# An encoder block's input stage: table times for the first eight tiles of x, two half tiles in other PSUM banks, copies of the first tokens moved

## The chip, the cores and the metric

The kernel runs on one core of a Trainium2 chip, as one program. The metric is the device time of one execution in microseconds (us), lower is better. Engines are named as in the profile: PE (TensorE; PEld its weight loads), DVE (VectorE), ACT (ScalarE), POOL (GpSimd), SP (SyncE, which issues all DMAs here).

## The reference

One encoder layer over x of 2048 tokens x 1024: a normalisation, one wide projection, two attention mixers, gates, three more projections. What the change touches is the first line, and the use of its result in the gate columns `ga`, `gb`:

```python
h = rms_norm(x, norm_gain)          # x * rsqrt(mean(x*x) + EPS) * gain
proj = h @ w_in
qa, ka, va, qb, kb, vb, ga, gb, mg = split(proj)
ya = banded_attention(...) * silu(ga)
yb = dilated_attention(...) * silu(gb)
gates = sigmoid(mg + b_merge)
y = x + (gates0 * (ya @ w_branch_a) + gates1 * (yb @ w_branch_b)) @ w_out
```

## The kernel before

**The input stage.** x is cut into 16 tiles of 128 tokens. Every matmul operand is split into a high and a low fp16 half, so that three fp16 products (high x high, low x high, high x low) stand for one fp32 product; the transposed x is kept in SBUF as `XH` and `XL` (1024 channels x tokens). A tile goes through these steps:

- `x_square` (L448, ACT): squares of the tile and their sum.
- `x_stats` (L452, L261, DVE; two small instructions) and `x_newton` (three Newton steps to the reciprocal root) for a group of tiles together. `rs_newton` makes nine small DVE instructions (L275 to L277) for the groups of two and twelve small POOL instructions (L270 to L273) for the groups of four. The groups are tiles 0-1, 2-3, 4-7, 8-11, 12-15.
- `x_scale` (L462, DVE): the tile (128x1024 fp32, SBUF to SBUF) times its factor.
- `x_turn` (L468, PE): four 128x128 transposes of a half tile (512 channels) into one of three PSUM banks "s". "(t,h)" below is half h of tile t; there are 32.
- `x_hi` (L471, ACT) copies the half tile from PSUM to fp16 `XH`; `x_lo` (L475, DVE) subtracts that from PSUM and writes `XL`.
- `x_again` (L479, POOL) copies the first two tiles' columns of `XH` and `XL` behind the last token (four copies).

**Beside it**, three column blocks of the gate weights (gate 0, 1, 2) are prepared: `g_gain` (L324, POOL, two halves), `g_square` (L332, ACT), `g_sum` (L194, PE), `g_pow` (L201 to L345, seven small DVE instructions), `g_hi` (L350, ACT), `g_lo` (L354, DVE); and the first unit's weights, with `w_gain` (L180, POOL, four quarters), `w_square` (L219, ACT) and others. `warm(n)` puts n matmuls of constants on PE (L502).

**The gates.** When the 512 tokens of quarter q (four tiles) are transposed, gates 0 and 1 of that quarter follow: 24 matmuls each (L308: `XH` by `gh`, `XL` by `gh`, `XH` by `gl` for eight channel blocks), then `tanh` (L371, ACT), `gate` (L378, DVE) and a store. Four quarters make 192 matmuls. Behind them begin the projections of the first unit (L651).

**What sets the order.** Every engine runs its own queue in order, and waits where an operand isn't ready. The program is recorded once on the host: `at(t, f)` puts step f on a heap under a planned time t, `until(t)` records all steps that are planned up to t, and `stream` records the 24 matmuls of a gate over 5.2 planned us with `until` between them. So the constants `X_...` are no waits: they only say in which order the instructions stand on each queue. In the version before, the planned time of a tile's scaling is a straight line in t, and everything of the tile hangs on it:

```python
def scale_time(t):
    return X_CH[0] + X_CH[1] * t
b = scale_time(t) + X_CH[2] + X_CH[5] * h
at(b, x_turn, t, h)
at(b + X_CH[3], x_hi, t, h)
at(b + X_CH[3] + X_CH[4], x_lo, t, h)
```

Of the kernel before, what the change touches and what calls it, by code (L numbers as in the profile page):

```python
# [32 lines left out]
NT = S // 128  # L33
# [47 lines left out]
Y_MAX = (0.026, 0.815, 0.839)  # L81
X_SQ = (5.098, 1.401, 9.779, 2.051)
X_CH = (9.3, 2.65, 1.024, 0.955, 1.155, 1.305)
X_ST = (1.3, 0.179)
X_G = (7.5, 15.282, 45.87)
X_GP = (2.1, 5.694, 7.094, 7.694, 8.894, 10.194)
X_W = (14.0, 38.0, 48.0, 1.1, 4.8, 5.2, 6.3, 0.6, 50.255)
X_WARM = (24, 16, 16, 16, 12)
X_TH = (0.8, 2.173, 3.5)
# [22 lines left out]
def block_kernel(tc, x, w_units, w_gate, w_mrg, w_brn, w_out, w_bra, gain, qkg, sink, bias_a, bias_b, b_merge, out):  # L112
# [326 lines left out]

    groups = {0: (0, 1), 1: (0, 1), 2: (2, 3), 3: (2, 3)}  # L440
    groups.update((t, tuple(range(t - t % 4, t - t % 4 + 4))) for t in range(4, NT))

# [21 lines left out]
    def x_turn(t, h):  # L464
        xps[t, h] = ps = s_p.tile([128, 4, 128], F32, name="s")
        for c in range(4):
            cc = 4 * h + c
            T.transpose(ps[:, c, :], xts[t][:, 128 * cc:128 * cc + 128], idf[:])  # L468

    def x_hi(t, h):  # L470
        A.activation(XH[:, 4 * h:4 * h + 4, 128 * t:128 * t + 128], xps[t, h][:], AF.Copy)  # L471

    def x_lo(t, h):
        ts = slice(128 * t, 128 * t + 128)
        V.tensor_tensor(XL[:, 4 * h:4 * h + 4, ts], xps[t, h][:], XH[:, 4 * h:4 * h + 4, ts], OP.subtract)  # L475
        done.add(("x", t, h))
# [35 lines left out]
    def scale_time(t):  # L512
        return X_CH[0] + X_CH[1] * t

    def ready_time(t):
        return scale_time(t) + sum(X_CH[2:])

    for t, n in enumerate(X_WARM):
        at(scale_time(t) + X_CH[2] - .05 if t < 4 else scale_time(3) + X_CH[2] + X_CH[5] + .05, warm, n)
    for t in range(NT):  # L520
        b = X_SQ[0] + X_SQ[1] * t if t < 4 else X_SQ[2] + X_SQ[3] * (t - 4)
        at(b, x_square, t)
        if t == groups[t][-1]:
            at(b + X_ST[0], x_stats, groups[t])
            at(b + X_ST[0] + X_ST[1], x_newton, groups[t])
        b = scale_time(t)
        at(b, x_scale, t)
        for h in range(2):
            b = scale_time(t) + X_CH[2] + X_CH[5] * h
            at(b, x_turn, t, h)  # L530
            at(b + X_CH[3], x_hi, t, h)
            at(b + X_CH[3] + X_CH[4], x_lo, t, h)
        if t < 2:
            for k in range(2):
                at(ready_time(t) + 1.0 + 1.2 * k, x_again, t, (XH, XL)[k])
        if t + XT_BUFS < NT:
            at(ready_time(t), x_load, t + XT_BUFS)
    for c in range(3):
        b = X_G[c]
        if c == 2:  # L540
            at(X_G[0] + X_GP[5] + .1, g_load, c)
        chain([(b + X_GP[0] * i, g_gain, c, i) for i in range(2)]
              + [(b + d, f, c) for d, f in zip(X_GP[1:], (g_square, g_sum, g_pow, g_hi, g_lo))])
    at(X_W[0], w_load, 0)
# [16 lines left out]
    for q in range(4):  # L561
# [1185 lines left out]
```

## Time and profile before

| | |
|---|---|
| time, median of 3 runs | 1960.59 us (1957.21 to 1961.2) |
| the profiled execution's own time | 1960.34 us |
| its span (first to last instruction) | 1958.6 us |
| busy: PE / DVE / ACT / POOL | 99% / 70% / 54% / 49% of the span |
| mean granted TensorE clock | 0.996 |
| first gate matmul, first matmul of the first unit | 28.60 us, 80.79 us after the span's start |

The profiled execution is 1.74 us longer than its span, and 0.25 us under the median. The busy shares are over the whole span; the change lies within its first 81 us, so what counts is what each engine waits for there.

### The profile page before, as it was taken

How to read it: one execution, taken by the hardware profiler on the slowest of the kernel's cores; microseconds unless marked ns; L12 is line 12 of the kernel's file. 1: busy time of each engine (PE TensorE's matmuls, PEld its weight loads, DVE VectorE, ACT ScalarE, POOL GpSimd, SP SyncE). 2: the span in 40 equal slices, each digit the busy share in tenths (PEclk: the TensorE clock that was granted, in tenths of full speed). 3: DMA queues.
4: the chain of work that ended last, by engine and by line, in shares of the span. 5: the costliest groups of instructions: out<-in, count | busy, mean ns of one | idle time of the engine just before them, and what ended most of it. 6: DMA issues, size and time to landing. Idle time of an engine off the chain costs nothing.

```text
span 1958.6 us, 48091 instructions
## 1 busy us (share of the span) xinstructions
PE 1935.7 (99%) x17606; PEld 1392.0 (71%) x17606; DVE 1377.4 (70%) x3604; ACT 1059.8 (54%) x2415; POOL 956.0 (49%) x2440
## 2 busy tenths in 40 slices
PE   8999999999999999999999999999999999999999
PEld 5567896677788898888989889899544444444444
DVE  6668777888768776667876878767776757876312
ACT  7457656776565566565666655656534545432100
POOL 4254556455546656647566676656511210232533
PEclk8999999999999999999999999999999999999999
DMA  6239987797848596677777776755822346788763
GB/s 250 81 81 168 194 150 159 141 187 141 177 101 184 118 185 126 125 148 164 152 132 154 135 169 126 143 118 118 187 81 85 106 165 195 218 241 268 252 228 145
DMA packets 589773, 308.46 MB, mean 157 GB/s; under 512 B 458080, under 2 KB 527328, under 8 KB 588256
## 3 DMA queue, kind: packets, MB, share of 16 engines
q1 hardware_dynamic: 589536, 305.39, 67.0%
q8 instruction: 137, 2.24, 0.5%
q14 instruction: 100, 0.82, 0.1%
HBM read 129.91 MB, written 65.27 MB: 100 GB/s over the span
## 4 chain that ended last, share of the span: by engine, by line
PE 80%; DVE 6%; POOL 6%; issue 4%; ACT 2%; DMA 2%; SPq 0%; POOLq 0%; DVEq 0%; ACTq 0%
PE pj L651 32%; PE pj L308 14%; PE fps L308 13%; PE fps L1614 7%; PE fps L1409 5%; PE s L805 4%; PE pv L854 4%; POOL rs_t L270 1%; DVE rw L715 1%; POOL rs_t L271 1%; DVE qss L703 1%; POOL rs_t L272 1%; POOL rw L722 1%; POOL rs_y L273 1%; PE pt L916 1%
## 5 line engine op out<-in xcount | busy, mean ns | idle before, releaser
L651 PE MATMUL pj<-wl,XH 128*128 128x128 f16 (+2 forms) x2816 | 715.2, 268 | 0.0
L651 PE MATMUL pj<-wh,XH 128*128 128x128 f16 (+2 forms) x2816 | 708.7, 268 | 4.0 <-DVE vt L691 4.0
L651 PE MATMUL pj<-wh,XL 128*128 128x128 f16 (+2 forms) x2816 | 711.6, 269 | 0.0
L651 PEld LDWEIGHTS <-XH 128*128 128x128 f16 x5632 | 574.6, 113 | 64.7 <-issue 5.8
L651 PEld LDWEIGHTS <-XL 128*128 128x128 f16 x2816 | 318.1, 113 | 26.7 <-issue 0.5
L820 DVE CUSTOM_DVE_ANT_0 pr<-s,b,ubuf 128x256 f32<-128x256 f32 (+3 forms) x512 | 218.6, 464 | 48.6 <-PE s L805 47.0
L270 POOL TENSOR_TENSOR rs_t<-rs_y 128x8 f32<-128x8 f32 (+2 forms) x345 | 105.4, 306 | 207.5 <-DVE rs_y L261 142.7
L837 DVE SCALAR_TENSOR_TENSOR p<-pr,p 128x512 f16<-128x512 f32 (+2 forms) x256 | 185.0, 723 | 21.6 <-ACT p L833 21.1
L308 PEld LDWEIGHTS <-wh 128*128 128x128 f16 x960 | 93.7, 98 | 111.0 <-issue 1.5
L715 DVE TENSOR_TENSOR rw<-rw,qr 128x512 f32<-128x512 f32 (+1 forms) x112 | 111.6, 997 | 86.7 <-POOL vt L678 58.4
L722 POOL TENSOR_TENSOR rw<-rw,g 128x128 f32<-128x128 f32 (+1 forms) x224 | 131.1, 605 | 78.1 <-DVE rw L715 62.1
L833 ACT ACTIVATE p<-pr 128x512 f16<-128x512 f32 (+2 forms) x256 | 159.5, 623 | 7.1 <-issue 0.3
L670 ACT ACTIVATE rw<-pj 128x256 f32<-128x256 f32 (+1 forms) x224 | 86.5, 386 | 134.3 <-PE pj L651 133.4
L737 POOL COPY spl<-spl 128x256 f16<-128x256 f16 (+1 forms) x224 | 93.7, 448 | 127.2 <-DVE spl L732 125.7
L308 PE MATMUL fps<-Y,wh 128*128 128x512 f16 x512 | 152.2, 379 | 0.0
L805 PE MATMUL s<-kq 128*128 128x128 f16 (+1 forms) x1856 | 147.3, 218 | 1.5 <-DMA kq<-spl 1.4
L805 PEld LDWEIGHTS <-kq 128*128 128x128 f16 x2016 | 129.8, 98 | 25.1 <-issue 2.0
L308 PE MATMUL pj<-XH,gh 128*128 128x512 f16 x384 | 145.5, 379 | 0.0
L308 PE MATMUL pj<-XH,gl 128*128 128x512 f16 x384 | 145.5, 379 | 0.0
L308 PE MATMUL pj<-XL,gh 128*128 128x512 f16 x384 | 145.5, 379 | 0.0
L1614 PE MATMUL fps<-wt,M 128*128 128x512 f16 (+1 forms) x684 | 145.2, 375 | 0.0
L728 ACT ACTIVATE spl<-rw 128x512 f16<-128x512 f32 (+1 forms) x112 | 72.1, 644 | 126.2 <-POOL vt L678 87.0
(241 smaller groups left out, 3702.2 us busy)
## 6 DMA issues: line engine op xcount, KB each, us to landing
wraw<-in_w_units_dram SPq DMA_DIRECT2D x56, 384.0 KB, 4.6
mtd<-mm SPq DMA_DIRECT2D x56, 256.0 KB, 3.7
M<-mtd SPq DMA_DIRECT2D x8, 1792.0 KB, 9.5
mgd<-fg SPq DMA_DIRECT2D x39, 256.0 KB, 2.1
zd<-z SPq DMA_DIRECT2D x128, 66.0 KB, 1.9
zz<-zd SPq DMA_DIRECT2D x64, 132.0 KB, 2.9
xt<-in_x_dram SPq DMA_DIRECT2D x16, 512.0 KB, 8.9
gtd<-yo SPq DMA_DIRECT2D x32, 256.0 KB, 2.7
```

The costliest lines, as they stand in the source:

```text
L270: G.tensor_tensor(tv, yv, yv, OP.mult)
L308: out.append(lambda w=w, xx=xx, ch=ch, i=i: T.matmul(ps[:], lhsT=w[:, ch, c0:c0 + 128], rhs=xx[:, ch, ts], start=(i == 0), stop=(i == n - 1)))
L651: out.append(lambda lhs=lhs, rhs=rhs, ch=ch, a=a, b=b, k=k: T.matmul(ps[:, a:b], lhsT=lhs[:, ch, :], rhs=rhs[:, ch, a:b], start=(k == 0), ...
L715: V.tensor_tensor(q, q, self.rr[:, :n].unsqueeze(2).to_broadcast([128, n, HD]), OP.mult)
L722: G.tensor_tensor(q[:, i, :un.nq, :], q[:, i, :un.nq, :], g, OP.mult)
L737: G.tensor_copy(sp[:, i, nh:, :, :], sp[:, i, nq:nh, ::-1, :])
L805: T.matmul(self.sv[j][:, o:o + k1 - k0], lhsT=q[:, h, :], rhs=kt[:, un.nq + kh + v * un.nk, k0:k1], start=(v == 0), stop=(v == 1))
L820: V.tensor_tensor_reduce(out=self.pv[:, j, self.p0:self.p0 + W], in0=self.sv[j], in1=un.bias[:, self.h0 + j, self.b0:self.b0 + W], scale=I ...
L833: A.activation(self.sp[:, :128 * n], self.pr, AF.Copy, scale=PSC)
L837: V.scalar_tensor_tensor(self.sp[:, 128 * n:], self.pr, PSC, self.sp[:, :128 * n], OP.mult, OP.subtract)
L1409: mm.append(lambda ch=ch, k=k, w=w, i=i: T.matmul(ps[:], lhsT=weight(bl, ch)[w], rhs=xblock(x, ch)[k], start=(i == 0), stop=(i == 11)))
L1614: mm.append(lambda ch=ch, k=k, w=w, i=i: T.matmul(ps[:, :cols.stop - cols.start], lhsT=m[:, a, ch, k, :], rhs=wt[w][:, b, ch, cols], start ...
```

## The change

The straight line is replaced by tables for the tiles 0 to 7: `X_SQ`, `X_SC`, `X_NW`, `X_TU`, `X_HI`, `X_LO` give each step a planned time of its own; tiles 8 to 15 follow a line again, with other constants. Tiles 4-5 and 6-7 become groups of two, whose Newton steps stay on POOL (`g[0] > 2`). The half tiles (1,1) and (2,0) are transposed into the two banks "pj", in which the gates accumulate later. The four `x_again` copies get planned times behind the quarter 1 gates. The 84 `warm` matmuls become 86, of which 60 stand ahead of the first transpose. A gate's matmuls are recorded no earlier than its weights' planned time. Nothing that is computed changes.

```diff
--- before.py
+++ after.py
@@ -79,13 +79,22 @@
 N_PREP = (6.3, 7.15, 7.753)
 B_GAP = (0.25, 0.138, 0.231)
 Y_MAX = (0.026, 0.815, 0.839)
-X_SQ = (5.098, 1.401, 9.779, 2.051)
-X_CH = (9.3, 2.65, 1.024, 0.955, 1.155, 1.305)
-X_ST = (1.3, 0.179)
-X_G = (7.5, 15.282, 45.87)
-X_GP = (2.1, 5.694, 7.094, 7.694, 8.894, 10.194)
-X_W = (14.0, 38.0, 48.0, 1.1, 4.8, 5.2, 6.3, 0.6, 50.255)
-X_WARM = (24, 16, 16, 16, 12)
+X_SQ = (4.7, 6.0, 7.67, 9.519, 13.423, 20.123, 22.646, 24.708, 27.708, 1.508)
+X_SC = (9.358, 10.138, 12.938, 13.688, 24.438, 25.089, 28.349, 29.268, 39.768, 2.218)
+X_NW = (7.25, 10.067, 20.868, 26.596, 36.596, 45.765)
+X_TU = (10.2, 10.9, 11.6, 12.3, 13.8, 14.493, 15.2, 15.9)
+X_HI = (11.3, 12.649, 13.349, 14.068, 16.645, 17.245, 17.49, 18.804)
+X_LO = (14.5, 15.675, 16.352, 17.052, 19.152, 20.901, 20.452, 20.869)
+X_WARM = (60, 0, 6, 12, 8)
+X_WT = (-1.003, 11.5, 13.892, 16.492, 19.692)
+X_AGAIN = 48.907
+X_CH = (1.024, 0.955, 1.155, 1.238)
+X_ST = 1.7
+X_G0 = (9.8, 13.049, 14.349, 16.349, 18.756, 20.691)
+X_G1 = (14.336, 20.174, 22.209, 22.874, 23.774, 25.779)
+X_G2 = (46.672, 54.444, 55.393, 56.249, 57.893, 59.393)
+X_GD = 1.863
+X_W = (17.0, 38.0, 50.417, 1.1, 4.956, 7.803, 8.828, 3.203, 53.849)
 X_TH = (0.8, 2.173, 3.5)
 T_Y = (2.0, 0.8, 1.6, 1.5, 4.0, 26.0, 0.5, 1.3, 2.1, 1.6, 2.0)
 T_P = ((0, 0.0, 0.03), (1, 3.0, 50.0), (2, 56.0, 75.0), (3, 82.0, 102.0), (4, 108.5, 128.3))
@@ -437,8 +446,8 @@
         V.tensor_scalar(bmh[:], bmt[:], 0.5, None, OP.mult)
 
 
-    groups = {0: (0, 1), 1: (0, 1), 2: (2, 3), 3: (2, 3)}
-    groups.update((t, tuple(range(t - t % 4, t - t % 4 + 4))) for t in range(4, NT))
+    GROUPS = (0, 1), (2, 3), (4, 5), (6, 7), (8, 9, 10, 11), (12, 13, 14, 15)
+    groups = {t: g for g in GROUPS for t in g}
 
     def x_square(t):
         g = groups[t]
@@ -455,24 +464,26 @@
     def x_newton(g):
         ss, y = xss[g]
         xss[g] = sm.tile([128, 4], F32, name="xr")
-        rs_newton(ss, y, xss[g][:, :len(g)], len(g), len(g) > 2)
+        rs_newton(ss, y, xss[g][:, :len(g)], len(g), g[0] > 2)
 
     def x_scale(t):
         i = t - groups[t][0]
         V.tensor_scalar(xts[t][:], xts[t][:], xss[groups[t]][:, i:i + 1], None, OP.mult)
 
     def x_turn(t, h):
-        xps[t, h] = ps = s_p.tile([128, 4, 128], F32, name="s")
+        k = 2 * t + h
+        ps = pj_p.tile([128, 512], F32, name="pj") if k in (3, 4) else s_p.tile([128, 512], F32, name="s")
+        xps[t, h] = ps = ps[:].rearrange("p (a b) -> p a b", a=4)
         for c in range(4):
             cc = 4 * h + c
             T.transpose(ps[:, c, :], xts[t][:, 128 * cc:128 * cc + 128], idf[:])
 
     def x_hi(t, h):
-        A.activation(XH[:, 4 * h:4 * h + 4, 128 * t:128 * t + 128], xps[t, h][:], AF.Copy)
+        A.activation(XH[:, 4 * h:4 * h + 4, 128 * t:128 * t + 128], xps[t, h], AF.Copy)
 
     def x_lo(t, h):
         ts = slice(128 * t, 128 * t + 128)
-        V.tensor_tensor(XL[:, 4 * h:4 * h + 4, ts], xps[t, h][:], XH[:, 4 * h:4 * h + 4, ts], OP.subtract)
+        V.tensor_tensor(XL[:, 4 * h:4 * h + 4, ts], xps[t, h], XH[:, 4 * h:4 * h + 4, ts], OP.subtract)
         done.add(("x", t, h))
 
     def x_again(t, X):
@@ -510,37 +521,40 @@
     at(2.0, small_loads)
 
     def scale_time(t):
-        return X_CH[0] + X_CH[1] * t
+        return X_SC[t] if t < 8 else X_SC[8] + X_SC[9] * (t - 8)
 
     def ready_time(t):
-        return scale_time(t) + sum(X_CH[2:])
-
-    for t, n in enumerate(X_WARM):
-        at(scale_time(t) + X_CH[2] - .05 if t < 4 else scale_time(3) + X_CH[2] + X_CH[5] + .05, warm, n)
+        return X_LO[2 * t + 1] if t < 4 else scale_time(t) + sum(X_CH)
+
+    for t, n in zip(X_WT, X_WARM):
+        at(t, warm, n)
+    for k, g in enumerate(GROUPS):
+        at(X_NW[k], x_stats, g)
+        at(X_NW[k] + X_ST, x_newton, g)
     for t in range(NT):
-        b = X_SQ[0] + X_SQ[1] * t if t < 4 else X_SQ[2] + X_SQ[3] * (t - 4)
-        at(b, x_square, t)
-        if t == groups[t][-1]:
-            at(b + X_ST[0], x_stats, groups[t])
-            at(b + X_ST[0] + X_ST[1], x_newton, groups[t])
+        at(X_SQ[t] if t < 8 else X_SQ[8] + X_SQ[9] * (t - 8), x_square, t)
         b = scale_time(t)
         at(b, x_scale, t)
         for h in range(2):
-            b = scale_time(t) + X_CH[2] + X_CH[5] * h
-            at(b, x_turn, t, h)
-            at(b + X_CH[3], x_hi, t, h)
-            at(b + X_CH[3] + X_CH[4], x_lo, t, h)
+            if t < 4:
+                tu, hi, lo = (v[2 * t + h] for v in (X_TU, X_HI, X_LO))
+            else:
+                tu = b + X_CH[0] + X_CH[3] * h
+                hi = tu + X_CH[1]
+                lo = hi + X_CH[2]
+            at(tu, x_turn, t, h)
+            at(hi, x_hi, t, h)
+            at(lo, x_lo, t, h)
         if t < 2:
             for k in range(2):
-                at(ready_time(t) + 1.0 + 1.2 * k, x_again, t, (XH, XL)[k])
+                at(X_AGAIN + 4 * t + 2 * k, x_again, t, (XH, XL)[k])
         if t + XT_BUFS < NT:
-            at(ready_time(t), x_load, t + XT_BUFS)
-    for c in range(3):
-        b = X_G[c]
+            at(ready_time(t) + .05, x_load, t + XT_BUFS)
+    for c, ts in enumerate((X_G0, X_G1, X_G2)):
         if c == 2:
-            at(X_G[0] + X_GP[5] + .1, g_load, c)
-        chain([(b + X_GP[0] * i, g_gain, c, i) for i in range(2)]
-              + [(b + d, f, c) for d, f in zip(X_GP[1:], (g_square, g_sum, g_pow, g_hi, g_lo))])
+            at(X_G0[5] + .1, g_load, c)
+        chain([(ts[0] + X_GD * i, g_gain, c, i) for i in range(2)]
+              + [(b, f, c) for b, f in zip(ts[1:], (g_square, g_sum, g_pow, g_hi, g_lo))])
     at(X_W[0], w_load, 0)
     steps = [(X_W[2] + X_W[4], w_sum, 0), (X_W[2] + X_W[5], w_pow, 0)]
     for i in range(4):
@@ -564,6 +578,8 @@
         until(pos)
         assert all(("x", t, h) in done for t in range(4 * q, 4 * q + 4) for h in range(2))
         for c in range(2):
+            pos = max(pos, (X_G0, X_G1)[c][5] + .1)
+            until(pos)
             mm, after = g_step(c, q)
             pos = stream(pos, 5.2, mm)
             for k, f in enumerate(after):
```

The diff's tables only set an order. The first place where the prediction rests on it is DVE's queue (xt is the tile that is scaled, xr its group's factor, XL the low half of a transposed half tile). Before, from the factor of tiles 2-3 on:

```order
24 L277 SCALAR_TENSOR_TENSOR xr<-rs_t,rs_y 128x2
25 L462 TENSOR_SCALAR xt<-xt,xr 128x1024
26 L475 TENSOR_TENSOR XL<-s,XH 128x4x128 x2
27 L462 TENSOR_SCALAR xt<-xt,xr 128x1024
28 L475 TENSOR_TENSOR XL<-s,XH 128x4x128
29 L201 TENSOR_REDUCE wm_315<-pt 128x1
30 L202 TENSOR_SCALAR wm_315<-wm_315 128x1
```

and now, from the scaling of tile 1 on:

```order
16 L471 TENSOR_SCALAR xt<-xt,xr 128x1024
17 L284 TENSOR_TENSOR rs_t<-rs_y 128x2
18 L285 SCALAR_TENSOR_TENSOR rs_t<-rs_t,xss 128x2
19 L286 SCALAR_TENSOR_TENSOR rs_y<-rs_t,rs_y 128x2
20 L284 TENSOR_TENSOR rs_t<-rs_y 128x2
21 L285 SCALAR_TENSOR_TENSOR rs_t<-rs_t,xss 128x2
22 L286 SCALAR_TENSOR_TENSOR rs_y<-rs_t,rs_y 128x2
23 L284 TENSOR_TENSOR rs_t<-rs_y 128x2
24 L285 SCALAR_TENSOR_TENSOR rs_t<-rs_t,xss 128x2
25 L286 SCALAR_TENSOR_TENSOR xr<-rs_t,rs_y 128x2
26 L471 TENSOR_SCALAR xt<-xt,xr 128x1024 x2
27 L486 TENSOR_TENSOR XL<-s,XH 128x4x128 x2
```

Tile 1 is now scaled ahead of the nine Newton instructions of tiles 2-3, and tiles 2 and 3 right behind them. Before, tile 1 was scaled behind those instructions (row 25), tile 2 behind two XL of tile 0 (row 27), and tile 3 at row 39. The g_lo of gate 0 comes at row 40 of the queue before, at row 38 now.

The second place is POOL's queue, where a group's factor xr is followed by the next step. Before, behind the factor of tiles 12-15:

```order
49 L271 TENSOR_TENSOR rs_t<-rs_t,xss 128x4
50 L272 TENSOR_SCALAR rs_t<-rs_t 128x4
51 L273 TENSOR_TENSOR xr<-rs_t,rs_y 128x4
52 L180 TENSOR_TENSOR wraw<-wraw,gn 128x768 x4
53 L324 TENSOR_TENSOR graw<-graw,gn 128x512 x2
```

and now, behind the factor of tiles 6-7:

```order
31 L280 TENSOR_TENSOR rs_t<-rs_t,xss 128x2
32 L281 TENSOR_SCALAR rs_t<-rs_t 128x2
33 L282 TENSOR_TENSOR xr<-rs_t,rs_y 128x2
34 L189 TENSOR_TENSOR wraw<-wraw,gn 128x768
35 L279 TENSOR_TENSOR rs_t<-rs_y 128x4
```

and behind that of tiles 12-15:

```order
58 L280 TENSOR_TENSOR rs_t<-rs_t,xss 128x4
59 L281 TENSOR_SCALAR rs_t<-rs_t 128x4
60 L282 TENSOR_TENSOR xr<-rs_t,rs_y 128x4
61 L333 TENSOR_TENSOR graw<-graw,gn 128x512
62 L490 COPY XH<-XH 128x8x128
63 L490 COPY XL<-XL 128x8x128
```

A quarter of the unit's weights (wraw) now stands directly behind the factor of tiles 6-7 too, and likewise at row 47 behind that of tiles 8-11; half of gate 2's weights (graw) stands behind that of tiles 12-15, and the four copies come last. Before, one of the copies stood behind the factor of tiles 4-7 (row 27), and the next Newton steps behind that of tiles 8-11.

The third place is PE's queue at the end of quarter 1's gates. Before, one half tile stands between six gate matmuls:

```order
396 L308 MATMUL pj<-XH,gl 128x512
397 L308 LDWEIGHTS gh
398 L308 MATMUL pj<-XH,gh 128x512
399 L308 LDWEIGHTS gh
400 L308 MATMUL pj<-XL,gh 128x512
401 L308 LDWEIGHTS gl
402 L308 MATMUL pj<-XH,gl 128x512
403 L468 MATMUL s<-idf,xt 128x128 x4
```

and now, where quarter 1 ends and quarter 2 begins:

```order
378 L317 MATMUL pj<-XL,gh 128x512
379 L317 LDWEIGHTS gl
380 L317 MATMUL pj<-XH,gl 128x512
381 L479 MATMUL s<-idf,xt 128x128 x24
382 L317 LDWEIGHTS gh
383 L317 MATMUL pj<-XH,gh 128x512
384 L479 MATMUL s<-idf,xt 128x128 x4
```

Six half tiles, (9,1) to (12,0), follow each other without a gate matmul between them; ahead of them, 33 of quarter 1's 48 gate matmuls stand with no transpose among them.

## Rows read from the trace of the kernel before

**Rows 1.** The page: span, and busy time of each engine.

```profile
span 1958.6 us, 48091 instructions
PE 1935.7 (99%) x17606; PEld 1392.0 (71%) x17606; DVE 1377.4 (70%) x3604; ACT 1059.8 (54%) x2415; POOL 956.0 (49%) x2440
```

**Rows 2.** Chain of waits in order of time: start us, us, what.

```profile
34.74 0.44 PE s L468 x4
...
70.41 10.38 PE pj L308 x48
80.79 7.81 PE pj L651 x48
```

**Rows 3.** Timeline of PE: start us, us, engine, line, operation, out<-in, count.

```profile
24.88 2.77 PE L502 MATMUL pv<-ones 128*128 128x256 f16 x12
...
29.03 0.38 PE L308 MATMUL pj<-XH,gl 128*128 128x512 f16 x1
...
56.44 0.38 PE L308 MATMUL pj<-XH,gh 128*128 128x512 f16 x1
```

**Rows 4.** Timeline of DVE.

```profile
12.03 0.96 DVE L261 TENSOR_SCALAR rs_y<-xss 128x2 int32<-128x2 int32 x1
13.03 0.16 DVE L275 TENSOR_TENSOR rs_t<-rs_y 128x2 f32<-128x2 f32 x1
...
14.67 0.75 DVE L462 TENSOR_SCALAR xt<-xt,xr 128x1024 f32<-128x1024 f32 x1
...
19.20 0.15 DVE L201 TENSOR_REDUCE wm<-pt 128x1 f32<-128x1 f32 x1
...
20.40 0.68 DVE L475 TENSOR_TENSOR XL<-s,XH 128x512 f16<-128x512 f32 x1
...
21.64 0.75 DVE L462 TENSOR_SCALAR xt<-xt,xr 128x1024 f32<-128x1024 f32 x1
22.30 1.28 DVE L354 SCALAR_TENSOR_TENSOR gl<-graw,ubuf,gh 128x1024 f16<-128x1024 f32 x1
23.50 1.28 DVE L475 TENSOR_TENSOR XL<-s,XH 128x512 f16<-128x512 f32 x2
26.50 1.49 DVE L462 TENSOR_SCALAR xt<-xt,xr 128x1024 f32<-128x1024 f32 x1 [1.72 <-POOL xr L273]
...
43.38 0.16 DVE L452 TENSOR_SCALAR xss<-xss 128x4 f32<-128x4 f32 x1
```

**Rows 5.** Timeline of POOL.

```profile
10.93 2.04 POOL L324 TENSOR_TENSOR graw<-graw,gn 128x512 f32<-128x512 f32 x2 [9.62 <-DMA graw<-in_w_gate_dram]
...
24.01 0.20 POOL L273 TENSOR_TENSOR rs_y<-rs_t,rs_y 128x4 f32<-128x4 f32 x1
...
26.26 0.20 POOL L273 TENSOR_TENSOR xr<-rs_t,rs_y 128x4 f32<-128x4 f32 x1
26.40 1.04 POOL L479 COPY XL<-XL 128x1024 f16<-128x1024 f16 x1
...
43.82 0.20 POOL L270 TENSOR_TENSOR rs_t<-rs_y 128x4 f32<-128x4 f32 x1 [5.59 <-DVE rs_y L261]
...
45.22 0.69 POOL L271 TENSOR_TENSOR rs_t<-rs_t,xss 128x4 f32<-128x4 f32 x1
...
47.55 1.47 POOL L180 TENSOR_TENSOR wraw<-wraw,gn 128x768 f32<-128x768 f32 x1
```

**Rows 6.** Timeline of ACT.

```profile
35.86 0.69 ACT L371 ACTIVATE yo<-pj,ubuf 128x512 f32<-128x512 f32 x1
...
39.17 1.05 ACT L448 ACTIVATE jk<-xt 128x1024 f16<-128x1024 f32 x1
...
40.41 0.60 ACT L471 ACTIVATE XH<-s 128x512 f16<-128x512 f32 x1
```

**Rows 7.** Busy time by stretch: PE, PEld, DVE, ACT, POOL (instructions), granted clock, DMA share, GB/s.

```profile
22.00:24.00 2.00, 0.63 (x4) 0.42 (x4) 2.00 (x3) 2.00 (x5) 1.76 (x3) 1.00 1.04 391
...
25.00:28.00 3.00, 2.65 (x13) 1.50 (x11) 1.50 (x2) 1.63 (x3) 2.02 (x7) 0.50 1.02 385
40.00:80.00 40.00, 40.00 (x223) 22.74 (x222) 30.80 (x73) 24.07 (x42) 11.60 (x20) 1.00 0.09 34
```

## The prediction

> **What bounds the kernel now.** I read the page first: PE is busy for 1935.7 of 1958.6 us [rows 1], so the time is PE's work plus what PE waits, and this change leaves PE's work as it is but for two `warm` matmuls. Then the chain of waits [rows 2]: from 34.74 us on it names PE itself, through the last 48 gate matmuls (10.38 us, so 0.216 each) to the first unit's at 80.79. The stretch from 40 to 80 us says the same: PE is busy for 40.00 of 40.00 us at a granted clock of 1.00 [rows 7]. So once the gates run, no half tile is late in the kernel before; it can gain at their start alone.
>
> The start shows in PE's timeline [rows 3]: the third gate matmul, the first that needs `g_lo`, is at 29.03. DVE's timeline [rows 4] shows why: `g_lo` (22.30, 1.28 us) is followed by two XL and a scaling of 1.49 us at 26.50, which waited 1.72 us for POOL's factor. POOL's [rows 5] shows that a scaling costs 0.75 us alone, but 1.49 when POOL's copy is issued 0.14 us behind the factor (26.26 and 26.40): it ended at 27.99, 0.55 behind that copy's end at 27.44. This pair of rows carries the forecast.
>
> Behind the gates both versions have the same order on every queue, and SP's queue is the same throughout. What the end of the gates gains or loses goes into the time one for one.
>
> **The change, part by part.** Prices: gate matmul 0.216; half tile 0.44 [rows 2]; scaling 0.75, the next DVE instruction 0.66 behind its start; XL 0.68, next 0.60 (two 1.28); `g_lo` 1.28, next 1.20; nine DVE Newton instructions 1.64 (13.03 to 14.67); seven `g_pow` 1.20 (19.20 to 20.40) [rows 4]. On POOL, eight Newton instructions take 2.25 (24.01 to 26.26), so twelve to the factor's end 11 x 0.28 + 0.24 = 3.33; they start 0.44 behind their `x_stats` (43.38 on DVE, 43.82 on POOL) [rows 4, 5].
>
> *A. The start.* The int32 instruction at 12.03 ends at 12.99 because POOL's gate gains run until 12.97; that stays. From there DVE's new order is: tile 1's scaling to 13.65, Newton to 15.29, tiles 2 and 3 to 16.61, two XL to 17.89, `g_pow` to 19.09, four XL to 21.65, `g_lo` to 22.93. Third gate matmul: **23.0** instead of 29.03, 6.0 earlier. One half tile fewer (8 instead of 9) is turned ahead of the gates, which puts 0.44 behind them: **-5.6**. If PE never waited afterwards, that would be the whole effect.
>
> *B. The waits behind it.* Tiles 4-7 now need two rounds of POOL's Newton steps, each between DVE's steps.
> - (6,0): `g_lo` leaves DVE at 22.85; 0.44; 3.33: factor of 4-5 at 26.6; two scalings and the second `g_lo` to 29.15; 0.44; 3.33: factor of 6-7 at 32.9. A quarter of the unit's weights (1.47, row at 47.55) is issued 0.1 ahead of that end and ends at 34.3; the scaling of tile 6 then ends 0.55 later, 34.85. PE is there after 37 further gate matmuls and four halves, 23.0 + 7.99 + 1.76 = 32.75. **+2.1**.
> - (8,0): from 34.85 PE has nine gate matmuls and four halves to the end of (7,1), 38.55. Its XH stands on ACT behind tanh (0.69) and a square (1.24 to the next: 39.17 to 40.41) and takes 0.60 [rows 6]; tanh starts with the last gate matmul's end at 38.1, so XH ends at 40.65. XL 0.68, then 0.44, 3.33: factor at 45.1; behind it weights to 46.45, scaling of tile 8 to 47.0. PE is there at 38.55 + 33 x 0.216 = 45.7. **+1.3**.
> - (11,0): POOL has three weight quarters and a half of gate 2 in a row from 45.0. I take 1.25 for each of the scalings of tiles 9 and 10, nearer to the held 1.49 than to 0.75. DVE: output product 0.6, tile 9, two XL (the second waits for (8,1) and ends at 50.4), tile 10 to 51.7, XL, statistics, product and XL to 53.9, tile 11 to 54.65. PE, with 15 gate matmuls and six halves from 47.0, is there at 52.85. **+1.8**.
> - (12,0): the statistics of 12-15 come at 52.4; 0.44; 3.33, and 0.49 for one of the twelve that is held itself (45.22: 0.69 instead of 0.20 [rows 5]): 56.65. Half of gate 2 (1.02) is issued behind it: 57.55, and the scaling ends at 58.1. PE is there at 54.65 + 0.88 = 55.55. **+2.5**.
>
> So quarter 2's first gate matmul comes at 58.1 + 0.44 = 58.55, against 56.44 [rows 3] with the same 96 gate matmuls and 25 half tiles done: +2.1, which agrees with -5.6 + 7.7.
>
> *C. The rest of the gates.* The four copies (1.04 each) now stand where tiles 13 and 14 are scaled, and ten small DVE instructions of the unit's weights ahead of later XL. Two held scalings at 0.55 to 0.74, partly covered by the matmuls between: **+1.0**, from 0 to 2.4.
>
> *D. The clock.* Between 51 and 58.5 us PE would have little but the six halves, 2.6 us. The trace has one such stretch: PE busy for 0.63 of the 2 us from 22 to 24, then a granted clock of 0.50 from 25 to 28, the 1.2 GHz level [rows 7], at which twelve `warm` matmuls took 2.77 [rows 3]. The same fall here would cost half of its 3 us: **+1.5**; 0 if the halves and the gates between are enough, 4 if it falls twice, as it may behind the start or behind (6,0).
>
> Sum: -5.6 + 7.7 + 1.0 + 1.5 = **+4.6** on the profiled execution's own 1960.34 (0.25 under the median of the runs, 1.74 over its span): **1965.0 us**.
>
> *What I cost at nothing.* The 60 `warm` matmuls ahead of the first transpose: even at 2.77/12 = 0.23 each they take 13.8 us, and the first half tile is needed at 16.6, when DVE comes to its XL; without that cover the start moves with them. The two halves in the "pj" banks: their XL ends at 21.1, ahead of the first accumulation. The copies' own place: only later units read them, and they end before the gates do. Gate 1's gains: their weights land too late to be moved ahead (the same rows of SP's queue).
>
> *The Trainium skill against the rows.* The Trainium skill ("SBUF — State Buffer", section "Who interferes with whom") says that DVE and GpSimd share a port pair, that whoever issues first holds it for the whole instruction, and that the other is fully blocked. The row at 26.50 agrees in kind, but the scaling ended 0.55 behind the copy's end, not its whole 0.75. By the rule taken strictly, five held scalings would each end 0.2 later, 1.0 in all, and the sum would be +5.6; the row decides, and I stay at 0.55.
>
> **The rivals.**
> 1. *POOL's instruction behind a factor doesn't hold the scaling*, or DVE gets in first. For it: the issue gap is only 0.14. Against: 26.50 shows one case that was held, and nothing else. Then the scalings end 0.75 behind the factor, and the waits are 0.9, 0.1, 1.0 and 2.1: -5.6 + 4.1 = -1.5, **1958.9**; with D, 1960.4. Chance 0.15.
> 2. *PE never waits again* (the other side): the start's gain stays whole, -5.6, **1954.7**. Its place is (12,0): it decides whether tile 12's scaling ends by about 51, when PE would be there without any wait, instead of at 58.1. That needs POOL's Newton rounds to begin earlier, that is the statistics not bound by XL(7,1) and XL(9,0) on DVE. Against it: their order on DVE's queue is fixed, and each round costs 3.33 us at least. Part of it (waits of 1 to 2 us) makes about -4, still over 0.2%. Chance 0.12.
> 3. *The waits come, the clock doesn't fall*: -5.6 + 7.7 + 1.0 = +3.1, **1963.4**. For it: between the waits PE does real matmuls. Chance 0.17.
> 4. *The clock falls also behind the start or (6,0)*: 0.50 granted there doubles every gate matmul for 3 us or more, which delays PE, though part of it only fills the wait that follows: +7 to +9, **1968.0**. Chance 0.13.
>
> That the change doesn't start the gates earlier is a rival too: if a tile of x or a gate's weights landed later than before, 23.0 would be missed. SP's queue is unchanged, so I give it no chance of its own.
>
> **How the numbers follow.** The forecast has 0.43. A measurement of this kernel can tell about 0.2%, 3.9 us, from no change. Faster than 1956.7 is only rival 2: 0.12. Within it are rival 1 (0.15), most of rival 3 (0.12), and the forecast's low end, where C and D cost little (0.06): 0.33. Slower than 1964.5 are the rest of the forecast (0.37), rival 4 (0.13), and rival 3 with C's upper end (0.05): 0.55. The range runs from rival 1 less some 1.4 for waits that I put too high, 1957.5, to rival 4 with C's upper bound, 1969.5; outside lie rival 2 (0.12) and the heaviest of rival 4 (0.05). The likeliest case alone spans 1963 to 1968.
>
> **What would show it.** PE's timeline: third gate matmul at 23.0; waits of 2.1, 1.3, 1.8 and 2.5 us ahead of (6,0), (8,0), (11,0) and (12,0); quarter 2 from 58.5; first unit from 85.4 instead of 80.79. DVE's: scalings of 1.2 to 1.9 us behind the factors of tiles 6-7, 8-11, 12-15, each ending some 0.5 behind a POOL instruction's end. By stretch: a granted clock of 0.50 right behind 58. I am wrong in B if those scalings take 0.75, wrong in D if the clock stays at 1.00, and wrong altogether if the first unit starts ahead of 80.

## The result, and the profile after

The changed kernel took 1965.7 us (median of 14 runs, 1961.56 to 1967.0), the kernel before 1960.43 (14 runs beside it). The ratio is 1.0026, with a 95% interval of 1.0018 to 1.0034: slower by 3.5 to 6.7 us. Forecast: 1965.0, slower by 4.6.

The profiled execution of the changed kernel is one of its three shortest, 1961.79 us, so a second profile (e1, 1964.71) stands beside it below. Its page, with the span and the busy time of each engine, is the counterpart of [rows 1]:

```profile
span 1959.7 us, 48111 instructions
...
PE 1933.3 (99%) x17608; PEld 1390.8 (71%) x17608; DVE 1381.1 (70%) x3606; ACT 1059.6 (54%) x2415; POOL 952.6 (49%) x2452
```

PE's timeline (start us, us, what, and in brackets the idle time ahead with what ended it) is the counterpart of [rows 3]:

```profile
22.25 0.38 PE L317 MATMUL pj<-XH,gl 128*128 128x512 f16 x1
...
31.98 0.38 PE L317 MATMUL pj<-XH,gl 128*128 128x512 f16 x1
33.95 0.63 PE L479 MATMUL s<-idf,xt 128*128 128x128 f32 x4 [1.60 <-DVE xt L471]
...
44.57 0.38 PE L317 MATMUL pj<-XH,gl 128*128 128x512 f16 x1
46.13 0.63 PE L479 MATMUL s<-idf,xt 128*128 128x128 f32 x4 [1.17 <-DVE xt L471]
...
50.70 1.47 PE L479 MATMUL s<-idf,xt 128*128 128x128 f32 x12
53.72 1.16 PE L479 MATMUL s<-idf,xt 128*128 128x128 f32 x8 [1.55 <-DVE xt L471]
57.00 1.08 PE L479 MATMUL s<-idf,xt 128*128 128x128 f32 x4 [2.11 <-DVE xt L471]
57.87 0.63 PE L317 MATMUL pj<-XH,gh 128*128 128x512 f16 x1
...
83.19 0.33 PE L667 MATMUL pj<-wh,XH 128*128 128x384 f16 x1
```

The gates start 6.8 us earlier than before, then PE waits four times, each time for a scaling, ahead of (6,0), (8,0), (11,0) and (12,0). Quarter 2 begins 1.4 later than before (57.87 against 56.44). The first unit's weights meet PE at 83.19, 2.56 later than in the kernel before, whose row is this:

```profile
80.63 0.33 PE L651 MATMUL pj<-wh,XH 128*128 128x384 f16 x1
```

From 57.00 on, a half tile takes 1.08 instead of 0.63 and a gate matmul 0.63 instead of 0.38. The rows by stretch show why (stretch, its length, PE's busy time with its instructions, granted clock, DMA share, GB/s):

```profile
54.00:58.00 4.00, 1.89 (x13) 0.88 0.00 0
58.00:61.00 3.00, 3.00 (x14) 0.60 0.00 0
61.00:65.00 4.00, 4.00 (x26) 1.00 0.00 0
```

The same stretches of the kernel before are at 1.00 throughout. The scalings that ended the waits, on DVE:

```profile
31.87 1.93 DVE L471 TENSOR_SCALAR xt<-xt,xr 128x1024 f32<-128x1024 f32 x1 [1.53 <-POOL xr L282]
...
44.05 1.93 DVE L471 TENSOR_SCALAR xt<-xt,xr 128x1024 f32<-128x1024 f32 x1 [3.40 <-POOL xr L282]
...
55.34 1.51 DVE L471 TENSOR_SCALAR xt<-xt,xr 128x1024 f32<-128x1024 f32 x1 [0.57 <-POOL xr L282]
```

and what POOL issued right behind the factor of tiles 6-7 and of tiles 12-15:

```profile
31.64 0.20 POOL L282 TENSOR_TENSOR xr<-rs_t,rs_y 128x2 f32<-128x2 f32 x1
31.79 1.47 POOL L189 TENSOR_TENSOR wraw<-wraw,gn 128x768 f32<-128x768 f32 x1
...
55.11 0.20 POOL L282 TENSOR_TENSOR xr<-rs_t,rs_y 128x4 f32<-128x4 f32 x1
55.26 1.04 POOL L333 TENSOR_TENSOR graw<-graw,gn 128x512 f32<-128x512 f32 x1
```

The two end at 33.26 and 56.30, the scalings at 33.80 and 56.85: 0.54 and 0.55 behind, as in the pair of [rows 4, 5].

### The profile page after: what moved, and what is told of

Read it like the earlier page. It is cut to its first block, busy times and chain, and to the rows that moved or that the text cites. A ratio compares the mean times of both kernels' runs of the same rounds, so it can differ in the third digit from the quotient of the medians.

```text
span 1959.7 us, 48111 instructions
## 1 busy us (share of the span) xinstructions
PE 1933.3 (99%) x17608; PEld 1390.8 (71%) x17608; DVE 1381.1 (70%) x3606; ACT 1059.6 (54%) x2415; POOL 952.6 (49%) x2452
## 4 chain that ended last, share of the span: by engine, by line
PE 80%; DVE 7%; POOL 6%; issue 4%; DMA 2%; ACT 2%; SPq 0%; POOLq 0%; DVEq 0%; ACTq 0%
PE pj L667 32%; PE pj L317 13%; PE fps L317 13%; PE fps L1630 7%; PE fps L1425 5%; PE s L821 4%; PE pv L870 4%; POOL rs_t L279 1%; DVE rw L731 1%; POOL rs_t L280 1%; POOL rs_t L281 1%; DVE qss L719 1%; POOL rw L738 1%; POOL rs_y L282 1%; PE pt L932 1%
## 5 line engine op out<-in xcount | busy, mean ns | idle before, releaser
L279 POOL TENSOR_TENSOR rs_t<-rs_y 128x8 f32<-128x8 f32 (+3 forms) x348 | 103.6, 298 | 217.7 <-DVE rs_y L270 148.3
```

The source lines that it names most:

```text
L279: G.tensor_tensor(tv, yv, yv, OP.mult)
```

## The experiments

Each kernel ran beside the kernel before on the same chip; ratios are to that. The part behind the first unit's start took 1875.0 to 1879.4 us in the profiled executions (span less that start), without an order among the kernels that explains it. So a profile tells where the first unit starts, and only the runs tell what an edit is worth in the time.

**e1, the changed kernel again.**

> The changed kernel once more, unedited. Its profiled execution took 1961.79 us where the median of its runs is 1965.7; the first unit began at 83.19 us, 2.4 later than before. Theory W (waits and clock in the input stage): most executions lose some 2 to 4 us more there, because the granted clock also falls to 0.50 behind another wait ((6,0) or the start), so a profile of such an execution shows the first unit near 85 to 87 us and a second stretch at 0.50 ahead of 60 us. Rival L (later): the first unit stands near 83.2 again, and the missing 2 to 4 us lie behind it. Ratio to the kernel before 1.002 to 1.003 by both.

Measured: 1964.49 us (11 runs), ratio 1.0020 (1.0011 to 1.0029). Its profile, PE's timeline and then stretches (columns as above):

```profile
21.50 2.51 PE L513 MATMUL pv<-ones 128*128 128x256 f16 x20
23.84 0.38 PE L317 MATMUL pj<-XH,gh 128*128 128x512 f16 x1
...
24.28 0.38 PE L317 MATMUL pj<-XH,gl 128*128 128x512 f16 x1
...
58.72 0.63 PE L479 MATMUL s<-idf,xt 128*128 128x128 f32 x4 [2.12 <-DVE xt L471]
...
84.91 0.33 PE L667 MATMUL pj<-wh,XH 128*128 128x384 f16 x1
```

```profile
17.00:20.00 3.00, 3.00 (x17) 0.50 1.04 412
20.00:23.00 3.00, 2.73 (x19) 0.70 1.01 401
...
58.00:61.00 3.00, 2.28 (x11) 0.73 0.00 0
61.00:65.00 4.00, 4.00 (x20) 0.78 0.00 0
```

W holds for the larger part. The spans of the two profiles differ by 2.8: 1.7 lie ahead of the first unit, which is at 84.91, 4.28 behind the kernel before, and 1.1 behind its start. The 1.7 come from the start, where the third gate matmul is 2.0 later. The waits behind it are nearly the same (1.34, 1.19, 1.54, 2.12); the first takes up 0.3 of the later start.

Not all of the 2.0 is the clock. The first profile and then e1, POOL's first gains of gate 0, and in e1 the first of DVE's `g_pow`:

```profile
10.22 2.04 POOL L333 TENSOR_TENSOR graw<-graw,gn 128x512 f32<-128x512 f32 x2 [8.92 <-DMA graw<-in_w_gate_dram]
```

```profile
10.73 2.04 POOL L333 TENSOR_TENSOR graw<-graw,gn 128x512 f32<-128x512 f32 x2 [9.43 <-DMA graw<-in_w_gate_dram]
...
18.58 0.16 DVE L210 TENSOR_REDUCE wm<-pt 128x1 f32<-128x1 f32 x1 [0.85 <-PE pt L203]
```

The weights landed 0.51 later in e1, ahead of any fall of the clock. Then, with the clock at 0.50, DVE waited for PE's `g_sum`, so `g_lo` came 1.45 later in all (22.18 against 20.73). The last 0.6 are the 20 constant matmuls, which ended after `g_lo`.

**e2, POOL waits for the first scaling.**

```diff
+    def x_pause(t):
+        pz = sm.tile([128, 1], F32, name="pz")
+        G.tensor_copy(pz[:], xts[t][:, :1])
...
         at(b, x_scale, t)
+        if t in (6, 8, 12):
+            at(b + .01, x_pause, t)
...
-        chain([(ts[0] + X_GD * i, g_gain, c, i) for i in range(2)]
+        chain([(ts[0] + (X_GD + .15 * (c == 2)) * i, g_gain, c, i) for i in range(2)]
```

> A one-column POOL copy that reads the scaled tile stands behind the factors of tiles 6-7, 8-11 and 12-15, so POOL's next large instruction starts only when the first scaling is done; nothing else is moved but half of gate 2's gain by one step. Theory H (that instruction holds the scaling): the scalings behind the three factors take 0.75 instead of 1.93, 1.93 and 1.51 us; the wait ahead of (6,0) falls from 1.60 by 1.2 to about 0.4, that of (8,0) from 1.17 to about 0, (12,0) from 2.11 to about 1.4; the tiles behind them are still held by the train of weights, so some 0.5 comes back. First unit 2.0 earlier than in the unedited kernel of the same chip, time 1.5 to 2.5 lower, ratio to before about 1.0015. Rival N (the scaling itself was slow, or the factor late whatever follows it): waits and time as in the unedited kernel, ratio 1.0026.

Measured: 1963.18 us, ratio 1.0010 (1.0002 to 1.0019), against 1964.49 for e1 on the same chip. DVE's scaling of tile 6 and the next one, then PE's half (6,0) and the first unit:

```profile
31.86 0.75 DVE L471 TENSOR_SCALAR xt<-xt,xr 128x1024 f32<-128x1024 f32 x1 [1.55 <-POOL xr L282]
...
33.13 1.70 DVE L471 TENSOR_SCALAR xt<-xt,xr 128x1024 f32<-128x1024 f32 x1
```

```profile
32.76 0.63 PE L483 MATMUL s<-idf,xt 128*128 128x128 f32 x4 [0.43 <-DVE xt L471]
...
82.55 0.33 PE L673 MATMUL pj<-wh,XH 128*128 128x384 f16 x1
```

H holds: the scaling starts at the same time and takes 0.75; 1.17 of the 1.60 ahead of (6,0) were the hold, 0.43 the late factor. The weights, only pushed behind, hold the next scaling instead (1.70).

The first unit is at 82.55, 2.36 ahead of e1, where I had expected 2.0. But most of that is e1's later start: ahead of the first profile, which has the same start (third gate matmul at 22.21 and 22.25), it is only 0.64. The waits behind the start are 2.1 shorter in all (4.29 against 6.43), but the clock is low for longer: 0.50 from 54 to 58 and 0.61 from 58 to 61, against 0.88 and 0.60. The intervals of e1 and e2 overlap. So that the hold makes these waits is shown; what it is worth in the time is not.

**e3, constant matmuls in the four waits.**

```diff
+FILL = {(6, 0): 13, (8, 0): 9, (11, 0): 12, (12, 0): 17}
...
+            if (t, h) in FILL:
+                at(tu - .001, warm, FILL[t, h])
             at(tu, x_turn, t, h)
```

> Constant matmuls (13, 9, 12 and 17 of them, about 0.11 us each) stand ahead of the half tiles (6,0), (8,0), (11,0) and (12,0), where PE waits 1.60, 1.17, 1.55 and 2.11 us; they need nothing that PE waits for. Theory C (the clock costs 1.5 to 4 us of the loss): the granted clock stays at 1.00 from 30 us to the first unit, the half tiles come at the same times as in the unedited kernel up to (12,0), and the first unit comes 1 to 3 us earlier; ratio to before 1.0005 to 1.002. Rival (the clock costs nothing, since the half tiles behind it wait for DVE anyway): the clock stays at 1.00 but the first unit stays where it was within 0.5 us, ratio 1.0026.

Measured: 1961.34 us, ratio 1.0001 (0.9992 to 1.0009), 3.2 us below e1 on the same chip. Stretches, and PE's timeline:

```profile
54.00:58.00 4.00, 3.73 (x33) 1.00 0.00 0
58.00:61.00 3.00, 2.72 (x16) 1.00 0.02 5
```

```profile
53.76 1.16 PE L480 MATMUL s<-idf,xt 128*128 128x128 f32 x8 [0.23 <-DVE xt L472]
57.04 0.63 PE L480 MATMUL s<-idf,xt 128*128 128x128 f32 x4 [0.27 <-DVE xt L472]
...
59.47 0.63 PE L480 MATMUL s<-idf,xt 128*128 128x128 f32 x4 [0.28 <-DVE xt L472]
...
82.04 0.33 PE L670 MATMUL pj<-wh,XH 128*128 128x384 f16 x1
```

The half tiles come when they came (53.76 and 57.04 against 53.72 and 57.00), so no wait is gone, yet the first unit is 1.15 earlier than in the first profile, which has the same start. C holds.

Why 1.15? In the first profile the two half tiles and four gate matmuls from 57.00 to 60.43 take 3.43 us; at 0.44 and 0.216 each they would take 1.74, so the low clock cost 1.69 there. In e3 a new wait takes some of that back: (13,0), at 59.47, waits 0.45 from the end of the slot before for the held scaling of tile 13 (1.30 in both profiles). The low clock had covered this wait.

That the runs gain 3.2 isn't fully accounted for: the two spans differ by 2.7, of which 1.55 lie behind the first unit's start, and the rest is not in these profiles.

**e4, earlier statistics.**

```diff
-X_SQ = (4.7, 6.0, 7.67, 9.519, 13.423, 20.123, 22.646, 24.708, 27.708, 1.508)
-X_SC = (9.358, 10.138, 12.938, 13.688, 24.438, 25.089, 28.349, 29.268, 39.768, 2.218)
-X_NW = (7.25, 10.067, 20.868, 26.596, 36.596, 45.765)
+X_SQ = (4.7, 6.0, 7.67, 9.519, 13.423, 20.123, 22.646, 23.7, 27.708, 1.508)
+X_SC = (9.358, 10.138, 12.938, 13.688, 24.438, 25.089, 28.349, 29.268, 38.768, 1.8)
+X_NW = (7.25, 10.067, 20.868, 24.4, 33.63, 39.0)
...
-X_W = (17.0, 38.0, ...
+X_W = (17.0, 49.0, ...
...
-                tu = b + X_CH[0] + X_CH[3] * h
+                tu = b + X_CH[0] + X_CH[3] * h + 3.0 * (t >= 12)
```

> The statistics of tiles 6-7, 8-11 and 12-15 stand earlier on DVE's queue (tile 7's square ahead of gate 1's high half on ACT), the unit's weights on POOL behind all factors, tiles 8 to 15 are scaled in steps of 1.8 instead of 2.218 planned us, and tiles 12 to 15 are transposed later than their scaling by 3. The start is that of the changed kernel. Theory W (Newton rounds that begin too late, and what stands behind the factors, eat the start's gain): no wait ahead of (6,0) and (8,0), at most 2 us of waits in all around (11,1), no fall of the clock behind 30 us, first unit at 76 to 77.5, which is 3 to 4 us ahead of the kernel before; ratio 0.998 to 0.9985. Rival S (DVE, ACT and POOL together can't supply the half tiles any faster): waits of 5 us or more stay in other places, first unit at 81 or later, ratio 1.0005 or above.

Measured: 1957.71 us, ratio 0.9986 (0.9977 to 0.9995): faster than the kernel before and the changed one. No wait ahead of (6,0) to (12,0) is left; the longest are these, and the first unit comes 1.9 ahead of the kernel before, 1.2 to 2.7 behind what I expected, with the start at 23.09 and the clock at 0.60 from 17 to 20:

```profile
52.95 0.38 PE L317 MATMUL pj<-XL,gh 128*128 128x512 f16 x1 [1.09 <-DVE XL L486]
...
62.59 0.66 PE L479 MATMUL s<-idf,xt 128*128 128x128 f32 x4 [1.25 <-DVE XL L486]
...
78.73 0.33 PE L667 MATMUL pj<-wh,XH 128*128 128x384 f16 x1
```

**e10 and e12, two parts of e4 alone**: `X_SQ[7]` and `X_NW` (e10), `X_W[1]` (e12).

> Of e4 only the earlier statistics (tile 7's square, and the four numbers of the statistics' times); the weights stay on POOL among the factors, and tiles 8 to 15 keep their times. Theory (both the late Newton rounds and what stands right behind the factors make the waits): the wait ahead of (6,0) is gone; those of (8,0), (11,0) and (12,0) stay at 1.5 to 2 us each, since weights and half of gate 2 still hold the scalings there and the train of them delays tiles 9 to 11; the clock still falls once behind 50 us; first unit at 81 to 82.5, ratio 1.0000 to 1.0012. Rival (the statistics' place is all): waits as in e4, 2.7 us in all, ratio 0.999 or below.

> The other half of e4 alone: the unit's weights go behind all factors on POOL (one number), the statistics and the times of tiles 8 to 15 stay as in the changed kernel. Theory: the scalings of tiles 6, 8, 9 and 10 are held no more (0.75 instead of 1.93, 1.93, 1.35 and 0.97), the waits ahead of (6,0) and (8,0) fall to 0.4 and 0.7, but the same 5.9 us of weights now hold the scalings and XL of tiles 12 to 15, with new waits of 0.7 to 1.2 us each ahead of (13,0), (14,0) and (15,1); first unit within 1.2 us of the unedited kernel, ratio 1.0015 to 1.003. Rival (the weights' place is what e4 gained by): first unit at 80 or earlier, ratio 0.9995 or below.

Measured: e10 1961.86 us, ratio 1.0015 (1.0006 to 1.0024); e12 1966.37, ratio 1.0037 (1.0024 to 1.0049). In e10 the wait ahead of (6,0) is gone and those of (8,0), (11,0), (12,0) are 1.64, 1.71 and 1.26, first unit at 81.23; the clock behind 50 us did not fall in its profile, which I had wrong, and the ratio is above my 1.0012. In e12 the first two waits fell to 0.41 and 0.75, but the one below came, and the clock was 0.50 from 54 to 58, so it is worse than I said:

```profile
66.63 0.66 PE L479 MATMUL s<-idf,xt 128*128 128x128 f32 x4 [1.76 <-DVE XL L486]
...
86.14 0.33 PE L667 MATMUL pj<-wh,XH 128*128 128x384 f16 x1
```

Neither part gives e4's gain alone. As I read the two profiles, early factors need POOL free behind them, and POOL free there only moves its 5.9 us of weights onto the last tiles unless the factors are early. That isn't shown: e4 also spaced tiles 8 to 15 otherwise, which was tried neither by itself nor taken out of e4.

**e5, constant matmuls at the start; e11, with e3's as well.**

```diff
-X_WARM = (60, 0, 6, 12, 8)
-X_WT = (-1.003, 11.5, 13.892, 16.492, 19.692)
+X_WARM = (60, 14, 10, 9, 3)
+X_WT = (-1.003, 11.5, 13.75, 15.85, 19.692)
```

In e11 `X_WARM` is (60, 16, 11, 10, 12), and `FILL` of e3 is added.

> The changed kernel with its constant matmuls ahead of the gates placed otherwise: 14, 10 and 9 of them in the three places where PE waits between 10 and 20 us (1.95, 1.33 and 1.24 us), and 3 instead of 20 right ahead of the first gate. In the second profile of the changed kernel the clock was 0.50 from about 16 to 22 us, the 20 ended at 23.84, and the third gate matmul came at 24.28 instead of 22.25. Theory K (the clock at the start takes back a part of the start's 5.6): the clock stays at 1.00 from 10 to 30 us, the third gate matmul is at 22.2 to 23.0, the first unit 1 to 1.5 us ahead of that second profile (84.91), ratio to before about 1.0013. Rival (the start is DVE's chain, whatever the clock): third gate matmul as before between 22.2 and 24.3, ratio 1.0020 to 1.0026.

> The changed kernel with both sets of constant matmuls: those of e3 in the four waits behind the start, and those of e9 at the start. All its waits for half tiles stay, only the clock is held. Theory (of the loss against the kernel before, waits and the start's gain nearly cancel, and the clock makes the rest): clock 1.00 from 10 us to the first unit, third gate matmul 22.2 to 23.0, first unit at 81.5 to 82.5, that is 1 to 2 us behind the kernel before (80.63 to 80.79), ratio 0.9995 to 1.0005, which is at or a little below e3 (1.0001). Rival (the waits alone make the loss, and e3 was lucky): 1.0015 or above.

Measured: e5 1961.75 us, ratio 1.0015 (1.0006 to 1.0024); e11 1959.61, ratio 1.0007 (0.9999 to 1.0016). Both profiles have the clock at 1.00 from 10 to 30 us and the third gate matmul at 22.27 and 21.78; the first unit is at 83.11 and 81.69. Part of that is the landing of gate 0's weights again: POOL's first gains begin at 10.42 in e5 and at 9.90 in e11. From there to the third gate matmul it is 11.85 and 11.88, in the first profile 12.03 (22.25 - 10.22), in e1 13.55 (24.28 - 10.73). So the low clock, with the 20 constant matmuls behind it, cost e1's start some 1.5. How often that happens isn't known, e5's interval overlaps e1's and e11 is not below e3: what the start's clock is worth in the mean isn't shown.

**e6 and e7, one part undone each**: the copies at `ready_time(t) + 1.0 + 1.2 * k` again (e6); `k in ()` for `k in (3, 4)`, so no half goes to the banks "pj" (e7).

> One part undone: the four copies of the first tokens stand where the kernel before planned them, behind tiles 0 and 1, instead of behind quarter 1's gates. They are 4 x 1.03 us of POOL from about 18.7 on. Theory W: they contend with the second half of the start's DVE work and delay the Newton steps of tiles 4-5 by about 1 us, so third gate matmul 0.5 later, a new wait of about 1 ahead of (4,0), (6,0) as before; in return the scalings of tiles 13 and 14 are held no more (1.30 and 1.04 us become 0.75). First unit within 0.7 us of the unedited one, ratio 1.0015 to 1.003. Rival (the copies beside the gates are what costs): first unit 2 us or more earlier, ratio 1.001 or below. Rival (the copies' move is most of the start's gain): third gate matmul at 26 or later.

> One part undone: the half tiles (1,1) and (2,0) go to the three banks s again. (1,1) then waits for the bank of (0,0), which the XL at 15.94 us frees at about 16.6, instead of standing at 13.5; its XH, and the XL behind it, come some 3 us later. Theory: third gate matmul at 25 to 26 (2.7 to 3 us later than in the unedited kernel with the same clock, more if the clock falls meanwhile), the waits behind it as before, since DVE's chain moves as a whole; first unit 2.5 to 3.5 later, ratio 1.0035 to 1.0045. Rival (the waits ahead of (6,0) and (8,0) take up the later start): first unit less than 1 us later, ratio below 1.003.

Measured: e6 1967.26 us, ratio 1.0046 (1.0033 to 1.0058); e7 1968.09, ratio 1.0051 (1.0037 to 1.0064). Both parts help, since each undone gives a ratio above e1's interval (1.0011 to 1.0029): the copies by more than I said, the banks by a little more. In e6 DVE's statistics of tiles 4-5 take 1.00 beside the last copy (0.17 in the first profile), the copy itself 2.03; their Newton steps on POOL begin at 24.21, and (4,0) waits (PE):

```profile
22.92 1.00 DVE L461 TENSOR_SCALAR xss<-xss 128x2 f32<-128x2 f32 x1
```

```profile
21.87 2.03 POOL L490 COPY XL<-XL 128x1024 f16<-128x1024 f16 x1
24.21 0.20 POOL L279 TENSOR_TENSOR rs_t<-rs_y 128x2 f32<-128x2 f32 x1 [0.31 <-ACT jk L457]
```

```profile
28.38 0.63 PE L479 MATMUL s<-idf,xt 128*128 128x128 f32 x4 [0.92 <-DVE xt L471]
```

The scalings of tiles 13 and 14 take 0.74 and 0.75, as expected. But the clock is at 0.50 from 58 to 61 and at 0.54 from 61 to 65, longer than in the first profile, which I hadn't expected.

In e7 (1,1) waits for its bank, the clock falls to 0.50 behind that, and the start comes 4 to 6 later than in the two profiles of the changed kernel instead of 3 (this execution took 1971.9 us, 3.8 above the median):

```profile
16.75 1.97 PE L479 MATMUL s<-idf,xt 128*128 128x128 f32 x8 [3.03 <-DVE XL L486]
...
28.23 0.38 PE L317 MATMUL pj<-XH,gl 128*128 128x512 f16 x1
```

The change's other parts, the two groups of two for tiles 4 to 7 and the new order of the start, were not undone by themselves.

**e8 and e9, e4 and e5 together**, with 12 (e8) or 14 (e9) constant matmuls behind (11,1); `X_WARM` is that of e5 in e8, that of e11 in e9.

> The earlier statistics of e4 and the start's constant matmuls of e5 together, and 12 constant matmuls behind (11,1), where e4 waited 0.33 and 1.09 us. Expected if the two terms add: clock 1.00 from 10 us to the first unit, third gate matmul 22.2 to 23.0, waits of real work of 2.5 us in all, first unit at 76 to 78 (e4: 78.73), ratio 0.9975 to 0.9982 (e4: 0.9986). If the start's clock costs nothing that DVE doesn't cost anyway: as e4, 0.9986.

> As e8, with 16, 11 and 10 constant matmuls in the three waits of the start, 12 instead of 3 right ahead of the first gate (there e8 waited 0.53 and 0.82 us and the granted clock fell to 0.50 for some 2 us from 22 us on), and 14 instead of 12 behind (11,1). Expected: clock 1.00 from 10 us to the first unit, third gate matmul 22.2 to 23.0, first unit at 77 to 78 (e8: 79.43, e4: 78.73), ratio to before 0.9972 to 0.9984. If the start's clock costs nothing: 0.9986 to 0.9989 again.

Measured: e8 1956.69 us, ratio 0.9989 (0.9981 to 0.9998); e9 1954.97, ratio 0.9982 (0.9973 to 0.9991), the fastest of all. With 3 constant matmuls ahead of the first gate e8 idled there and the clock was 0.64 from 23 to 27; with 12 it stayed at 1.00. The waits alone don't decide that: e5, with the same 3 and the same waits (0.53 and 0.82), stayed at 1.00. e9's timeline:

```profile
22.32 0.39 PE L317 MATMUL pj<-XH,gl 128*128 128x512 f16 x1 [0.53 <-DVE gl L363]
...
78.02 0.33 PE L669 MATMUL pj<-wh,XH 128*128 128x384 f16 x1
```

Between e4, e8 and e9 the intervals overlap; that each beats the kernel before, none reaching 1, is shown. e8 missed what I expected (0.9975 to 0.9982, first unit at 76 to 78; it is at 79.43), e9 met its 0.9972 to 0.9984. So that the start's constant matmuls add to e4's gain isn't shown.

## Why the prediction was right, step by step

The forecast's case came true: the gain of the start is more than eaten by waits behind POOL's factors, and the clock falls behind the last of them.

- **A, third gate matmul at 23.0, -5.6.** Measured 22.25 and 24.28, so -6.3 and -4.3. The first: gate 0's weights landed 0.71 earlier than in the profile of before (POOL's gains at 10.22 against 10.93), which is nearly all of the difference. The second: they landed 0.20 earlier, but with the clock at 0.50 `g_lo` ended at 23.46 only (22.18 + 1.28), and the third matmul came 0.8 behind that. I costed the 60 constant matmuls at nothing, which they were, and left out the 20 right ahead of the first gate, behind which the gates had to begin. That a landing moves though SP's queue is the same I gave no chance of its own; between the two profiles of one program it moved by 0.51.
- **B, 2.1, 1.3, 1.8 and 2.5.** From the end of the slot before (0.216 a gate matmul, 0.44 a half) the first profile gives 33.95 - 32.20 = 1.75, 46.13 - 44.79 = 1.34, 53.72 - 52.01 = 1.71 and 57.00 - 54.59 = 2.41: 7.2 where I had 7.7. The hold at 0.55 behind POOL's end was the right price (0.54, 0.55), and e2 shows it as a cause. By the Trainium skill ("SBUF — State Buffer", section "Who interferes with whom"), when DVE works in a two-port mode, whoever of DVE and GpSimd issues first blocks the other fully; the traces agree but for the 0.2 us by which a held scaling ends sooner.
- **C, +1.0 from the copies.** Wrong: the scalings of tiles 13 and 14 were held, 1.30 and 1.04, but no wait of PE stands behind (12,0) in the two profiles. Its lower end, 0, was the case, for a reason that the term doesn't have: the low clock of D covered it. At a clock of 1.00, in e3, (13,0) does wait for tile 13, for 0.45 (and likewise in e11, at 59.12). So C and D don't add as the sum has them.
- **D, +1.5 from the clock, right behind 58.** It fell at 57. "One such stretch" was a misreading: the trace of before has another, 4.70 us without work of PE ahead of 10.01 and then 0.50 from 10 to 14, which I passed over. What the first unit lost beyond A and B is 2.56 - (-6.34 + 7.2) = 1.7, and by the second profile 4.28 - (-4.31 + 7.0) = 1.6, where 7.0 is its four waits by the same count. The rows at the low clock give the first again: 1.69. e3's runs, with the clock held, are 3.2 shorter: more than the term, within its 0 to 4, but its profile shows only 1.15 of that ahead of the first unit.

So -6.3 or -4.3, +7.2 or +7.0, and +1.7 or +1.6 make the first unit 2.6 or 4.3 later; the median of the runs is nearer to the second. That the sum came within 0.7 us of the median is partly luck. C was too high where the second profile's start was worse than A, and the time behind the first unit's start, which the sum takes as unchanged, differs by 1.1 between the two profiles of the changed kernel and by up to 4.4 among all.

Rival 1 (no hold) fell by e2, rival 2 (no waits) by the four waits, rival 3 (no clock fall) by the profiles. Rival 4 was half there: the clock did fall at the start in e1, though the total was the forecast's.

## What to carry to other kernels

Pulling a start forward pays only as far as the supply behind it moves too: ask of each later group when its factor is ready, and what its engine issues right behind it. Here a large POOL instruction right behind a factor held DVE's scaling by it in all three places. Where PE must wait, constant matmuls that end inside the wait kept its clock for the work behind it (e3, e11); where they stood right ahead of the work, they were on the path as soon as the clock was low (e1). And a low clock can cover a wait that comes back when it is cured (e3).

## What the hardware showed

- The same program kept a clock of 1.00 at its start in one execution and was at 0.50 from 16 to 20 us in another (first profile and e1), and its gates then began 2.0 us apart, 0.5 of which is a later landing ahead of the fall. PE had waited 2.52 us ahead of (1,0) there, against 1.95. The Trainium skill ("TensorE: Matmul & The Clock Gate", section "Part 1: The HAM clock gate (the "warmup" mystery)") says that the number of slow matmuls at a kernel's start differs from run to run. These profiles show something near to it, not the same: both are at 1.00 in their first 5 us, and e1 falls later, behind waits.
- 51 constant matmuls, which compute nothing that is used, made the program 3.2 us faster by the medians (e3 against e1, ratios 1.0001 and 1.0020).
- A copy on POOL took 2.03 us instead of 1.04 in e6, from 21.87 on, beside DVE's work of the start (there `g_lo` took 1.65 instead of 1.28); that DVE held it, as POOL holds DVE, fits, but wasn't tried by itself.
